# Attention keys stored window by window, gate loads and bias set-up at other times, and the gate multiplied into half of the output weights

## The chip, the cores and the metric

The kernel runs on one core of one Trainium2 chip. The metric is device time in microseconds (us) of one execution, as the median of several runs. A profile is one further execution, recorded by the hardware profiler; it is read through views (groups of instructions by line, waits, timelines, sums over windows, the chain that ended last). The five engines are TensorE (PE; its weight loads are listed as PEld), VectorE (DVE), ScalarE (ACT), GpSimd (POOL) and SyncE (SP), whose queue issues most DMAs.

## What is computed

One layer of a backbone with three kinds of heads, for 1024 latent tokens (a grid of 16 rows x 64 columns), 256 context tokens and width 1024:

```
mod   = silu(c) @ w_ada + b_ada;  shift, scale, gate = split(mod, 3)
h     = rmsnorm(x, norm_g) * (1 + scale) + shift          # the same for ctx, with c_ctx
z     = h @ w_in                                          # 3840 columns, cut into 11 parts
ya    = z_b * conv3(z_c * z_h) * silu(z_g)                # 256 columns
yb    = attention(q, k, v, k_ctx, v_ctx, rpb) * silu(z_g) # 8 heads of 64
yc    = silu(layernorm(conv31(z_p * sigmoid(z_q)))) * silu(z_g)
out   = rmsnorm(x + gate * (concat(ya, yb, yc) @ w_out), final_g)
```

In the attention each latent query sees a clamped window of 8 rows x 16 columns of the grid, with a learned bias by head, row and column distance (rpb), and all 256 context keys, in one softmax with scale 1/8.

## The kernel before

**Arithmetic.** Every float32 operand of a large product is split into a high part, rounded to the fp32r type, and the rest (`split`, L129 and L130: the high part on ACT, the subtraction on POOL or DVE). A product is then three matmuls: high x high, high x low, low x high.

**Order of the work.** The program is Python that unrolls into one instruction list. PE's order is the order of the program text. In the first stage DVE, ACT, POOL and SP also follow the text; after it a scheduler orders these four, by the order of the text and its own estimate of when operands are ready. Each engine then executes its list strictly in order, waiting at the first instruction whose operands are missing.

- *Start (0 to 66 us).* The string `SEQ` is the written order: each word is a letter for a function in `start` with its arguments. `L` loads a part of w_ada, `X` a token tile, `W` half of a weight block of w_in, `w` splits it (`split_w`, ACT then POOL), `q`, `r`, `x` make the RMS norm, `B` multiplies by w_ada (L220), `R` copies that row out of PSUM (ACT, L225), `C` turns it into columns and makes scale and shift (PE transposes L232, DVE L234 to L240), `a`, `b`, `c` are PE transposes of normed tokens (L279), `f`, `g`, `h` apply scale and shift (ACT, L294), `u`, `v`, `o` split the result (DVE, L300 and L301), `m`, `n` are the query and key products of head pair 0 (L1009 to L1012), `Q` stores them, and `D` issues matmuls on zeros that keep PE going.
- *Values and set-up (66 to 163 us).* `build` runs the first conformer projection, the context keys of pair 0 and the value projection (`v_proj`, L412 to L414, ten tiles of 24 matmuls) on PE. Beside them run coroutines. `spawn(gen, delay)` adds one; `run` issues PE work and advances a planned clock `now` by an estimate for each product; `poll` lets those coroutines issue a step whose time has come. `v_weights` splits the value weights. `ada_gates` loads 16 pieces of the gate columns of w_ada (L809), sums them on DVE (L812, L814), splits the sum and stores it to DRAM (`gd`, L822). `bias_first` makes the bias tables of the first head: DMAs through DRAM (L445) into seven arrays `u`, then 21 loads into the tables `bt` (L502). `conv_part(31, 1.6)` issues the first 31 of 62 taps of the 31-wide convolution on DVE (L685). `drain()` issues all that is left before attention starts. The pool `t2` has four buffers: the loads and split halves of `ada_gates` and the value tiles that leave PSUM (ACT L423, DVE L424, stored by L425) take them in turn. PSUM holds three projection results (`ps_z`).
- *Attention (163 to 486 us).* For each of four head pairs: queries and keys are projected, then 16 blocks (2 heads x 8 blocks of 16 rows x 8 columns of queries) run with other projections in between. `sink_k` writes the keys times -1/8 into `kt[:, h]`, the high part in 64 partitions and the rest in the other 64 (ACT L371, DVE L372), token after token. `scores` multiplies a block of 128 queries by 2 or 3 column groups of keys (`kwin`, L589) and by the context keys (L590), twice each (queries high and low). The 256 or 384 window keys are read as 16 rows x 8 columns for each group: runs of 8 numbers, 64 apart.
- *Output (486 to 616 us).* `load_wout` loads a half of w_out (512 columns) in four pieces of 128x1024 through two buffers `fraw` and splits them (ACT, POOL; L130, tile `wol`). Half 0 is loaded first, then the y tiles, then half 1, all ahead of the output matmuls. `out_mm` makes 24 matmuls for a tile of 128 tokens (L867 to L869); the first four tiles of half 0 run on six of eight channel blocks first, then `gate_rows` broadcasts the gate row to all partitions (PE L836, DVE L838), then the rest. `out_part` multiplies a result by the gate (DVE L883), adds x (L884) and makes the sum of squares (ACT L890; DVE L886 for the last 256 columns); `out_gain` multiplies by final_g on POOL (L894); `out_mean` and `out_scale` make 1/rms on POOL (L900, L902, L909, L910) and scale and store the tile (L913 to L921).

Of the kernel before, what the change touches and what calls it, by code (L numbers as in the profile page):

```python
# [16 lines left out]
P = 128  # L17
D = 1024
# [33 lines left out]
X0 X1 X2 X3 L00 K L01 W00 W10 L10 L11 X4 X5 X6 X7 W01 W11 L20 L21 L30 L31 X8 X9  # L52
q00 q11 r02 q20 x0 x1 q31 r22 x2 x3 D29 B00 D02 B01 a0 R0 a1 w00 w10 C0 a22 D07
f0 f1 a3 u0 u1 m0 B10
# [7 lines left out]
def f32(ap):  # L62
    return ap.bitcast(F32)


class Builder:
# [236 lines left out]

    def load_w(self, src):
        return [w for g in range(2) for w in self.split_w(self.load_wraw(src, g))]

# [5 lines left out]

    def split_w(self, wr):
        hk = KT // 2
        wh = self.wp.tile([P, hk, P], F32R, name="wh", tag="wh")
        wl = self.wp.tile([P, hk, P], F32R, name="wl", tag="wl")
        self.split(wh, wl, wr, self.nc.gpsimd)
        return [(wh[:, i], wl[:, i]) for i in range(hk)]
# [17 lines left out]
    def proj_lat(self, c0, sink, ctx=False, w=None):  # L336
        if w is None:
            w = self.load_w(self.a["w_in"][:, c0:c0 + P])
            for half in range(2):
                yield from self.proj(w, half * HALF, HALF, lambda ps: sink(half, ps))  # L340
        if ctx:
            yield from self.proj(w, T, TC, lambda ps: sink(2, ps))
        yield 0
# [18 lines left out]

    def sink_k(self, half, ps, heads=(0, 1)):
        nc = self.nc
        t0, n = half * HALF, ps.shape[1]
        s = -QSCALE
        for h in heads:
            own = slice(64 * h, 64 * h + 64)
            oth = slice(64 - 64 * h, 128 - 64 * h)
            kk = self.kt[:, h, t0:t0 + n]  # L370
            nc.scalar.activation(out=kk[own], in_=ps[own], func=AF.Copy, scale=s)  # L371
            nc.vector.scalar_tensor_tensor(out=kk[oth], in0=ps[own], scalar=s, in1=f32(kk[own]),  # L372
                                           op0=ALU.mult, op1=ALU.subtract)

# [201 lines left out]
    def scores(self, kt, h, b, qv):  # L576
# [272 lines left out]

    def load_wout(self, half, pool):  # L850
        wh = pool.tile([P, KT, HALF], F32R, name=f"woh{half}")
        wl = pool.tile([P, KT, HALF], F32R, name=f"wol{half}")
        for q in range(4):
            raw = self.fr.tile([P, 2, HALF], F32, name="fraw")
            src = self.a["w_out"][q * 256:(q + 1) * 256, half * HALF:(half + 1) * HALF]
            self.nc.sync.dma_start(out=raw, in_=src.rearrange("(k p) n -> p k n", p=P))
            self.split(wh[:, 2 * q:2 * q + 2], wl[:, 2 * q:2 * q + 2], raw, self.nc.gpsimd)
        return wh, wl
# [18 lines left out]
    def out_part(self, tt, cs, j, ps, lp, eng):  # L877
# [4 lines left out]
        g = lp.tile([P, HALF], F32, name="fg", bufs=2)[:, 0:n]  # L882
        nc.vector.tensor_tensor(out=g, in0=ps[:, 0:n], in1=self.gate[:, cs], op=ALU.mult)  # L883
        nc.vector.tensor_tensor(out=xt[:, cs], in0=g, in1=xt[:, cs], op=ALU.add)  # L884
        if eng is nc.vector:
            nc.vector.tensor_tensor_reduce(g, xt[:, cs], xt[:, cs], op0=ALU.mult, op1=ALU.add, scale=1.0, scalar=0.0,  # L886
                                           accum_out=ss[:, j:j + 1])
        else:
# [16 lines left out]
    def out_scale(self, tt, j, parts):  # L905
        nc = self.nc
        xt, ss = self.xres[tt]
        r, s = ss[:, 3:4], ss[:, j - 1:j]
        nc.gpsimd.tensor_scalar(out=r, in0=ss[:, j:j + 1], scalar1=1.0 / D, scalar2=s, op0=ALU.mult, op1=ALU.add)  # L909
        nc.gpsimd.tensor_tensor(out=r, in0=r, in1=self.mhalf[:, 0:1], op=ALU.pow)  # L910
# [13 lines left out]
    def start(self, zb, attn_pool):  # L924
# [22 lines left out]

        def w(i, g):
            ws[i][4 * g:4 * g + 4] = self.split_w(wr.pop((i, g)))

# [80 lines left out]
    def build(self):  # L1031
# [53 lines left out]
        self.spawn(self.v_weights(stv.enter_context(self.pool("vw", 1, side="right"))), 2.0)  # L1085
        self.spawn(self.ada_gates(), 5.0)
        self.spawn(self.bias_first(), 10.0)
        first = self.cf_in(0)
        self.run(itertools.islice(first, KT), self.proj_pair(0, self.ws[1]), first)
        self.conv = self.cf_conv()  # L1090
        self.spawn(self.conv_part(31, 1.6))
        self.run(self.v_proj())
        self.drain()
        stv.close()
# [20 lines left out]
        with ExitStack() as st:  # L1115
# [76 lines left out]
```

## Time and profile before

| | |
|---|---|
| median of 3 runs | 619.52 us (618.75 to 619.55) |
| profiled execution, its own time | 617.89 us |
| span of its instructions | 616.1 us |
| instructions in the profile | 8935, of them 3101 matmuls |
| bytes read from and written to HBM | 55.93 MB and 14.29 MB |
| mean granted TensorE clock | 0.995 of full speed |

The profile's page gives, for each engine, the time in which it had an instruction under way, its share of the span and the count. The end of a matmul is modelled, and matmuls overlap, so the time from one start to the next says more than the duration. A row of a timeline reads: start, duration, engine, line, operation, out<-in, shape, count; in square brackets stands how long the engine sat idle before it and what it waited for. A row of a windows view gives each engine's busy time and count in a stretch, then the granted clock (PEclk), the busy share of the DMA engines and GB/s. A row of groups gives busy time, the mean in ns of one, and the idle time before them with the releaser.

### The profile page before, as it was taken

The page shows a single profiled execution, that of the slowest core. Times are in us where ns is not written, and L with a number is a line of the kernel's source. Part 1 is how long each engine was busy: PE and PEld are TensorE (multiplying, and loading weights), DVE is VectorE, ACT ScalarE, POOL GpSimd, SP SyncE. Part 2 cuts the span into 40 slices and gives each one's busy share as a digit, 9 for nine tenths or more (in the row PEclk, how much of TensorE's full clock was granted, in tenths as well). Part 3 has the DMA queues.
Part 4 walks back from the last instruction along what each step waited for, and adds up shares of the span by engine and source line. Part 5 has one row for each costly group of instructions (what it writes and reads, how often), then busy time and mean ns, then how long its engine had stood idle before and what let it go on. Part 6 is the DMA issues. An engine that isn't in the chain of part 4 may idle for free.

```text
span 616.1 us, 8935 instructions
## 1 busy us (share of the span) xinstructions
PE 593.8 (96%) x3101; PEld 497.0 (81%) x3101; DVE 401.1 (65%) x682; ACT 244.0 (40%) x468; POOL 178.4 (29%) x199
## 2 busy tenths in 40 slices
PE   7799999899999999999999999999999999999995
PEld 5467887688888888888888888888788888888884
DVE  4466977798356589577797666836879456352433
ACT  2455812111255542455523554424645434331222
POOL 1231112300233221424322433313434270265112
PEclk9999999899999999999999999999999999999998
DMA  8991658965623117331146242172311455770122
GB/s 286 357 326 41 222 151 175 158 173 160 164 49 93 37 55 202 75 86 49 28 136 141 48 113 55 36 222 52 82 28 35 133 151 160 273 272 1 70 102 103
DMA packets 97171, 78.64 MB, mean 128 GB/s; under 512 B 26508, under 2 KB 80870, under 8 KB 96998
## 3 DMA queue, kind: packets, MB, share of 16 engines
q1 hardware_dynamic: 95397, 71.51, 41.6%
q10 hardware_dynamic: 1728, 6.55, 3.0%
q8 instruction: 25, 0.41, 0.3%
q14 instruction: 21, 0.16, 0.1%
HBM read 55.93 MB, written 14.29 MB: 114 GB/s over the span
## 4 chain that ended last, share of the span: by engine, by line
PE 82%; DVE 6%; DMA 4%; ACT 2%; issue 2%; SPq 1%; POOL 1%; DVEq 0%; POOLq 0%; ACTq 0%
PE ps_z L324 13%; PE ps_z L326 13%; PE ps_z L325 13%; PE po L620 5%; PE ps_t L608 5%; PE ps_f L868 5%; PE ps_f L869 5%; PE ps_f L867 5%; PE ps_s L589 4%; DMA t<-in_w_ada 2%; PE ps_s L590 2%; PE ps_z L412 2%; PE ps_z L414 2%; PE ps_z L413 2%; DMA wa<-in_w_ada 2%
## 5 line engine op out<-in xcount | busy, mean ns | idle before, releaser
L324 PE MATMUL ps_z<-h,wh 128*128 128x512 f32 x384 | 151.1, 394 | 0.0
L326 PE MATMUL ps_z<-h,wl 128*128 128x512 f32 x384 | 150.2, 391 | 0.0
L325 PE MATMUL ps_z<-h,wh 128*128 128x512 f32 x384 | 149.7, 390 | 0.0
L130 POOL TENSOR_TENSOR wl<-wr,wh 128x512 fp32r<-128x512 f32 x52 | 71.8, 1384 | 146.8 <-ACT wh L129 118.0
L599 POOL TENSOR_SCALAR pr<-pr,sm 128x640 f32<-128x640 f32 (+1 forms) x64 | 52.9, 827 | 138.0 <-DVE sm L598 117.2
L326 PEld LDWEIGHTS ps_z<-h,wl 128*128 128x128 f32 x384 | 72.1, 188 | 16.1
L685 DVE SCALAR_TENSOR_TENSOR acc<-t,half_w,acc 128x1024 f32<-128x1024 f32 x60 | 83.0, 1384 | 1.0
L325 PEld LDWEIGHTS ps_z<-h,wh 128*128 128x128 f32 x384 | 72.2, 188 | 12.4
L324 PEld LDWEIGHTS ps_z<-h,wh 128*128 128x128 f32 x384 | 72.2, 188 | 12.1
L612 ACT ACTIVATE pw<-ps_t 128x640 fp32r<-128x640 f32 (+1 forms) x64 | 43.5, 680 | 90.7 <-PE ps_t L608 90.6
L594 DVE CUSTOM_DVE_ANT_0 ps_s<-ps_s,bt 128x640 f32<-128x640 f32 (+1 forms) x64 | 51.0, 796 | 33.7 <-PE ps_s L590 31.0
L613 DVE TENSOR_TENSOR pw<-ps_t,pw 128x640 fp32r<-128x640 f32 (+1 forms) x64 | 50.4, 788 | 17.3 <-ACT pw L612 16.9
L597 ACT ACTIVATE pr<-ps_s,mn 128x640 f32<-128x640 f32 (+1 forms) x64 | 49.0, 766 | 20.2 <-DVE mn L594 19.2
L620 PE MATMUL po<-pw,vt 128*128 128x256 f32 x304 | 51.3, 297 | 2.0 <-DVE yb L571 1.0
L868 PE MATMUL ps_f<-wol,y 128*128 128x512 f32 (+1 forms) x136 | 51.6, 379 | 0.0
L869 PE MATMUL ps_f<-woh,y 128*128 128x512 f32 (+1 forms) x136 | 51.5, 379 | 0.0
L867 PE MATMUL ps_f<-woh,y 128*128 128x512 f32 (+1 forms) x136 | 51.5, 379 | 0.0
L129 ACT ACTIVATE wh<-wr 128x512 fp32r<-128x512 f32 x52 | 32.5, 629 | 34.9 <-PE ps_z L325 20.9
L608 PE MATMUL ps_t<-ident,pr 128*128 128x128 f32 x304 | 43.6, 272 | 0.0
L620 PEld LDWEIGHTS po<-pw,vt 128*128 128x128 f32 x304 | 40.4, 189 | 3.8 <-issue 3.4
L589 PE MATMUL ps_s<-kt,qd 128*128 128x384 f32 (+1 forms) x128 | 42.2, 351 | 0.5 <-ACT pr L597 0.4
L608 PEld LDWEIGHTS ps_t<-ident,pr 128*128 128x128 f32 x304 | 36.0, 142 | 1.8 <-issue 0.9
(171 smaller groups left out, 911.4 us busy)
## 6 DMA issues: line engine op xcount, KB each, us to landing
wr<-in_w_in SPq DMA_DIRECT2D x52, 256.0 KB
wa<-in_w_ada SPq DMA_DIRECT2D x16, 512.0 KB
qd<-qn SPq DMA_DIRECT2D x32, 256.0 KB
vd<-t SPq DMA_DIRECT2D x20, 256.0 KB
x_in<-in_x SPq DMA_DIRECT2D x8, 512.0 KB
t<-in_w_ada SPq DMA_DIRECT2D x16, 256.0 KB
vt<-vd SPq DMA_DIRECT2D x32, 128.0 KB
fraw<-in_w_out SPq DMA_DIRECT2D x8, 512.0 KB
```

What stands on the lines that cost most here:

```text
L130: i2 = (eng or nc.vector).tensor_tensor(out=lo, in0=src, in1=f32(hi), op=ALU.subtract)
L324: nc.tensor.matmul(ps, lhsT=wh, rhs=hh, start=(k == 0), stop=False)
L325: nc.tensor.matmul(ps, lhsT=wh, rhs=hl, start=False, stop=False)
L326: self.last = nc.tensor.matmul(ps, lhsT=wl, rhs=hh, start=False, stop=(k == KT - 1))
L589: nc.tensor.matmul(win, lhsT=q[:, b % 4], rhs=kwin, start=(i == 0), stop=(i == 1))
L599: nc.gpsimd.tensor_scalar(out=pr, in0=pr, scalar1=sm, scalar2=0.5, op0=ALU.mult, op1=ALU.mult)
L608: nc.tensor.transpose(out=pt[:, c * P:(c + 1) * P], in_=pr[:, c * P:(c + 1) * P], identity=self.ident)
L620: self.nc.tensor.matmul(po, lhsT=vt[:, vi, h], rhs=pw[:, c], start=(c == 0), stop=(c == n - 1))
L685: self.after_pe(nc.vector.scalar_tensor_tensor(out=acc, in0=u[:, t:t + T], scalar=self.half_w[:, 2 * t + ct:2 * t + ct + 1], in1=acc, op0= ...
L867: nc.tensor.matmul(ps, lhsT=yh, rhs=wh[:, ch], start=(first and i == 0), stop=False)
L868: nc.tensor.matmul(ps, lhsT=yh, rhs=wl[:, ch], start=False, stop=False)
L869: nc.tensor.matmul(ps, lhsT=yl, rhs=wh[:, ch], start=False, stop=(last and i == len(chs) - 1))
```

## The change

1. **Keys.** `kt[:, h, 0:1024]` is stored group by group: eight groups of 128 keys, each 16 rows x 8 columns, so that `kwin` is one contiguous run. `sink_k` writes with that permutation. The factor -1/8 moves into the key weights: `split_w` applies it (ACT on the high part, then DVE in place of POOL for the rest); for pair 0 a further ACT instruction in `w` scales the raw weights.
2. **Start.** The first splits of the query and key weights (`w00 w10` in `SEQ`) become `w001`, placed ahead of `R0`, and `w101`, placed after `a1`; the last digit 1 sends their subtraction to DVE instead of POOL. `w01` and `w11` stay on POOL.
3. **Set-up.** `ada_gates` starts at 1.0 instead of 5.0 on the planned clock, `bias_first` at 22 instead of 10, the gap between convolution taps is 2.2 instead of 1.6, and the `drain()` after the value projection is gone.
4. **Output.** Half 1 of w_out is loaded after `gate_rows`, and each piece is multiplied in place by the gate on POOL before it is split. `out_part` of that half omits the multiplication on DVE. For the last 256 columns the sum of squares takes the earlier sum as its start value and 1/1024 as its scale, so that one POOL instruction of `out_scale` goes.

```diff
-q00 ... D29 B00 D02 B01 a0 R0 a1 w00 w10 C0 a22 D07
+q00 ... D29 B00 D02 B01 a0 w001 R0 a1 w101 C0 a22 D07
...
+    def split_w(self, wr, scale=None, eng=None):
         wh = self.wp.tile([P, hk, P], F32R, name="wh", tag="wh")
         wl = self.wp.tile([P, hk, P], F32R, name="wl", tag="wl")
-        self.split(wh, wl, wr, self.nc.gpsimd)
+        if scale is None:
+            self.split(wh, wl, wr, eng or self.nc.gpsimd)
+        else:
+            self.nc.scalar.activation(out=wh, in_=wr, func=AF.Copy, scale=scale)
+            self.nc.vector.scalar_tensor_tensor(out=wl, in0=wr, scalar=scale, in1=f32(wh), op0=ALU.mult, op1=ALU.subtract)
...
     def sink_k(self, half, ps, heads=(0, 1)):
-            kk = self.kt[:, h, t0:t0 + n]
-            nc.scalar.activation(out=kk[own], in_=ps[own], func=AF.Copy, scale=s)
-            nc.vector.scalar_tensor_tensor(out=kk[oth], in0=ps[own], scalar=s, in1=f32(kk[own]),
-                                           op0=ALU.mult, op1=ALU.subtract)
+            if half < 2:
+                kk = self.kt[:, h, 0:T].rearrange("p (g r c) -> p r g c", g=NB, c=BW)[:, 8 * half:8 * half + 8]
+                src = ps.rearrange("p (r g c) -> p r g c", g=NB, c=BW)
+            else:
+                kk, src = self.kt[:, h, T:], ps
+            nc.scalar.activation(out=kk[own], in_=src[own], func=AF.Copy)
+            nc.vector.tensor_tensor(out=kk[oth], in0=src[own], in1=f32(kk[own]), op=ALU.subtract)
...
-        kwin = kt[:, h, 0:T].rearrange("p (r g c) -> p g r c", g=NB, c=BW)[:, g0:g0 + ng]
+        kwin = kt[:, h, g0 * GK:(g0 + ng) * GK]
...
     def load_wout(self, half, pool, gate=None):
...
             self.nc.sync.dma_start(out=raw, in_=src.rearrange("(k p) n -> p k n", p=P))
+            if gate is not None:
+                self.nc.gpsimd.tensor_tensor(out=raw, in0=raw, in1=gate.unsqueeze(1).to_broadcast([P, 2, HALF]),
+                                             op=ALU.mult)
...
-        nc.vector.tensor_tensor(out=g, in0=ps[:, 0:n], in1=self.gate[:, cs], op=ALU.mult)
-        nc.vector.tensor_tensor(out=xt[:, cs], in0=g, in1=xt[:, cs], op=ALU.add)
+        if j == 0:
+            nc.vector.tensor_tensor(out=g, in0=ps[:, 0:n], in1=self.gate[:, cs], op=ALU.mult)
+            nc.vector.tensor_tensor(out=xt[:, cs], in0=g, in1=xt[:, cs], op=ALU.add)
+        else:
+            nc.vector.tensor_tensor(out=xt[:, cs], in0=ps[:, 0:n], in1=xt[:, cs], op=ALU.add)
...
+            nc.vector.tensor_tensor_reduce(g, xt[:, cs], xt[:, cs], op0=ALU.mult, op1=ALU.add, scale=1.0 / D,
+                                           scalar=ss[:, j - 1:j], accum_out=ss[:, j:j + 1])
...
+        def w(i, g, e=0):
+            t = wr.pop((i, g))
+            if i:
+                S.activation(out=t, in_=t, func=AF.Copy, scale=-QSCALE)
+            ws[i][4 * g:4 * g + 4] = self.split_w(t, eng=(G, V)[e])
...
-        self.spawn(self.ada_gates(), 5.0)
-        self.spawn(self.bias_first(), 10.0)
+        self.spawn(self.ada_gates(), 1.0)
+        self.spawn(self.bias_first(), 22.0)
...
-        self.spawn(self.conv_part(31, 1.6))
+        self.spawn(self.conv_part(31, 2.2))
         self.run(self.v_proj())
-        self.drain()
...
-            w1 = self.load_wout(1, lp)
...
                         self.gate_rows(ps_g)
+                        w1 = self.load_wout(1, lp, self.gate[:, HALF:])
```

More of the change, by code (lines that the diff above doesn't have):

```diff
@@ L52 @@
 X0 X1 X2 X3 L00 K L01 W00 W10 L10 L11 X4 X5 X6 X7 W01 W11 L20 L21 L30 L31 X8 X9
-q00 q11 r02 q20 x0 x1 q31 r22 x2 x3 D29 B00 D02 B01 a0 R0 a1 w00 w10 C0 a22 D07
+q00 q11 r02 q20 x0 x1 q31 r22 x2 x3 D29 B00 D02 B01 a0 w001 R0 a1 w101 C0 a22 D07
 f0 f1 a3 u0 u1 m0 B10
@@ L301, in h_split, with load_w @@
         nc.vector.tensor_tensor(out=lo, in0=raw, in1=f32(hi), op=ALU.subtract)
-    def load_w(self, src):
-        return [w for g in range(2) for w in self.split_w(self.load_wraw(src, g))]
+    def load_w(self, src, scale=None):
+        return [w for g in range(2) for w in self.split_w(self.load_wraw(src, g), scale)]
     def load_wraw(self, src, g):
@@ L311, in load_wraw @@
         return wr
-    def split_w(self, wr):
+    def split_w(self, wr, scale=None, eng=None):
         hk = KT // 2
@@ L337, in proj_lat @@
         if w is None:
-            w = self.load_w(self.a["w_in"][:, c0:c0 + P])
+            w = self.load_w(self.a["w_in"][:, c0:c0 + P], -QSCALE if ctx else None)
             for half in range(2):
@@ L364, in sink_k @@
         nc = self.nc
-        t0, n = half * HALF, ps.shape[1]
-        s = -QSCALE
         for h in heads:
@@ L848, in load_y, with load_wout @@
         self.split(*self.y[ch], raw)
-    def load_wout(self, half, pool):
+    def load_wout(self, half, pool, gate=None):
         wh = pool.tile([P, KT, HALF], F32R, name=f"woh{half}")
@@ L882, in out_part @@
         g = lp.tile([P, HALF], F32, name="fg", bufs=2)[:, 0:n]
-        nc.vector.tensor_tensor(out=g, in0=ps[:, 0:n], in1=self.gate[:, cs], op=ALU.mult)
-        nc.vector.tensor_tensor(out=xt[:, cs], in0=g, in1=xt[:, cs], op=ALU.add)
+        if j == 0:
[3 more added lines that the diff above has]
+            nc.vector.tensor_tensor(out=xt[:, cs], in0=ps[:, 0:n], in1=xt[:, cs], op=ALU.add)
         if eng is nc.vector:
-            nc.vector.tensor_tensor_reduce(g, xt[:, cs], xt[:, cs], op0=ALU.mult, op1=ALU.add, scale=1.0, scalar=0.0,
-                                           accum_out=ss[:, j:j + 1])
+            nc.vector.tensor_tensor_reduce(g, xt[:, cs], xt[:, cs], op0=ALU.mult, op1=ALU.add, scale=1.0 / D,
+                                           scalar=ss[:, j - 1:j], accum_out=ss[:, j:j + 1])
         else:
@@ L908, in out_scale @@
         r, s = ss[:, 3:4], ss[:, j - 1:j]
-        nc.gpsimd.tensor_scalar(out=r, in0=ss[:, j:j + 1], scalar1=1.0 / D, scalar2=s, op0=ALU.mult, op1=ALU.add)
+        if j == 1:
+            nc.gpsimd.tensor_scalar(out=r, in0=ss[:, j:j + 1], scalar1=1.0 / D, scalar2=s, op0=ALU.mult, op1=ALU.add)
+        else:
+            r = ss[:, j:j + 1]
         nc.gpsimd.tensor_tensor(out=r, in0=r, in1=self.mhalf[:, 0:1], op=ALU.pow)
@@ L946, in W @@
             wr[i, g] = self.load_wraw(a["w_in"][:, 1024 + 512 * i:1152 + 512 * i], g)
-        def w(i, g):
-            ws[i][4 * g:4 * g + 4] = self.split_w(wr.pop((i, g)))
+        def w(i, g, e=0):
[3 more added lines that the diff above has]
+            ws[i][4 * g:4 * g + 4] = self.split_w(t, eng=(G, V)[e])
         def q(i, e):
@@ L1132, in build @@
             ps_g = e(self.pool("ps_g", 2, PSUM, side="right"))
-            w1 = self.load_wout(1, lp)
             self.xres = []
             sync, act, half0 = nc.sync.dma_start, nc.scalar.dma_start, slice(0, HALF)
-            for half, w in ((0, w0), (1, w1)):
+            w = w0
+            for half in range(2):
+                if half:
+                    w = w1
                 for t0 in (0, 4):
```

## The prediction, made before the change was run

> **What bounds the kernel now.** I read the page first, then sums over stretches of the span, then PE's waits.
>
> ```profile
> span 616.1 us, 8935 instructions
> PE 593.8 (96%) x3101; PEld 497.0 (81%) x3101; DVE 401.1 (65%) x682; ACT 244.0 (40%) x468; POOL 178.4 (29%) x199
> 526.00:616.00 90.00, 83.11 (x385) 68.65 (x383) 34.03 (x49) 21.98 (x45) 30.20 (x38) 0.98 0.38 138
> ```
>
> PE is the bound: it is idle for 616.1 - 593.8 = 22.3 us in all. So there are only two ways to gain: take away PE's idle time, or make its own instructions shorter. In the third row (stretch, length, then busy time of PE, PEld, DVE, ACT, POOL) 6.9 us of the idle time lie in the output; the other engines work there after the last matmul. PE's waits name two more that this change can reach:
>
> ```profile
> PE ps_z L412 <- DVE t L424: 3.1, 1, 3.1
> PE ps_h L279 <- ACT h_raw L294: 1.2, 1, 1.2
> ```
>
> **Set-up: the 3.1 us wait.** The timeline of PE around it, and the sum of that stretch:
>
> ```profile
> 106.15 0.40 PE L414 MATMUL ps_z<-wv,h 128*128 128x512 f32 x1
> 109.66 0.47 PE L412 MATMUL ps_z<-wv,h 128*128 128x512 f32 x1 [3.11 <-DVE t L424]
> ...
> 110.89 0.51 PE L414 MATMUL ps_z<-wv,h 128*128 128x512 f32 x1
> ...
> 114.54 0.40 PE L414 MATMUL ps_z<-wv,h 128*128 128x512 f32 x1
> 114.77 0.40 PE L412 MATMUL ps_z<-wv,h 128*128 128x512 f32 x1
> 106.00:115.00 9.00, 5.89 (x19) 4.37 (x18) 8.96 (x11) 2.17 (x5) 2.10 (x1) 0.81 0.96 188
> ```
>
> At full clock a 512-wide matmul starts 0.23 us after the one before (the last pair). From 106.15 to 109.66 is 3.51 us: 3.28 lost. From 110.89 to 114.54 are nine starts in 3.65 us instead of 2.07: 1.58 more lost, since the granted clock falls after the stall (mean 0.81 in this stretch). The wait costs 4.86 us, not 3.1.
>
> Its cause, followed back: a value tile could not leave PSUM, since the gate's chain held its `t2` buffer.
>
> ```profile
> 95.21 3.26 SPq L809 DMA_DIRECT2D t<-in_w_ada  x1
> 101.16 0.75 DVE L814 SCALAR_TENSOR_TENSOR acc<-t,stat,acc 128x512 f32<-128x512 f32 x1 [2.46 <-DMA t<-in_w_ada]
> 106.07 0.39 ACT L423 ACTIVATE t<-ps_z 128x256 fp32r<-128x256 f32 x1 [1.75 <-DMA gd<-t]
> L814 DVE SCALAR_TENSOR_TENSOR acc<-t,stat,acc 128x512 f32<-128x512 f32 x14 | 11.2, 815 | 7.6 <-DMA t<-in_w_ada 7.5
> ```
>
> A value tile is 24 x 0.23 = 5.5 us of PE and the third ends at 106.4, so the first was ready at 95.4; it moves at 106.07, after the gate's store. The last gate load is issued at 95.21 and the last sum starts at 101.16. The 14 sums lose 7.5 us to loads that share SP's queue with the bias DMAs. The change starts the gate four planned microseconds earlier (4.2 us of real time: the text plans 0.65 for three matmuls that take 0.69), moves the bias DMAs 12.7 us back, out of the loads' way, and thins the taps on DVE. So the chain moves by 4.2 to 4.2 + 7.5 = 11.7 us, and the buffers come free at 94.4 to 101.9 instead of 106.07. PE needs its fourth `ps_z` at 106.4, and a value half leaves PSUM by steps of 0.4 us on ACT and DVE: it fits at both ends, with 2 us to spare at the worse one. I take all of it, -4.9; if some stall stays and only the after-effect goes, it is -1.6. The gate's sums now stand ahead of the splits of the value weights on DVE, which is in order: a split can wait behind a gate load as L814 did, 2.46 us. The splits are for tiles that PE reaches at 90 at the earliest, so the price is 0 as long as the loads keep the pace.
>
> The bias DMAs are moved past the value stores, on SP.
>
> ```profile
> 156.31 1.35 SPq L359 DMA_DIRECT2D qd<-qn  x2
> ```
>
> The first queries were issued at 156.31 at 0.68 us each; attention will want them 4.9 us earlier. From 106 to 151 the text issues on SP 18 value stores, 7 loads into `u`, 21 into the tables, 9 of values and some 6 others: 61 x 0.68 = 41 us of 45. That just fits, so I cost it at nothing; without that cover PE waits for the queries (rival 2). POOL's fills for the tables move with them, ahead of nothing that PE needs. Some seven taps move beside the gate projection and the first attention blocks, on a DVE that is busy 65% of the span: nothing.
>
> **Start: -0.6 us.**
>
> ```profile
> 17.74 1.14 ACT L129 ACTIVATE wh<-wr 128x512 fp32r<-128x512 f32 x2
> 18.44 2.53 POOL L130 TENSOR_TENSOR wl<-wr,wh 128x512 fp32r<-128x512 f32 x2 [5.47 <-ACT wh L129]
> 18.98 0.76 DVE L238 TENSOR_TENSOR scl<-ada_t,modc 128x4 f32<-128x4 f32 x1
> 19.77 1.22 DVE L240 TENSOR_TENSOR scl<-scl,modc 128x4 f32<-128x4 f32 x1
> 21.09 1.45 ACT L294 ACTIVATE h_raw<-ps_h,shift,scl 128x512 f32<-128x512 f32 x2 [2.21 <-DVE scl L240]
> 23.42 0.69 DVE L301 TENSOR_TENSOR h<-h_raw,h 128x512 fp32r<-128x512 f32 x1
> 28.45 0.16 DVE L240 TENSOR_TENSOR scl<-scl,modc 128x4 f32<-128x4 f32 x1
> ```
>
> L238 and L240 handle four numbers a partition and took 0.76 and 1.22 us while POOL ran its two subtractions; at 28 us, with POOL idle, L240 took 0.16. With the subtractions on DVE the two lose 1.66 us. Against it: ACT gets a third step (1.14 / 2 = 0.57), one cast now ahead of `R0`, and DVE gets a subtraction (0.69, as L301) ahead of the reduction. The second weight half had landed by 18.3, when its cast ran. If it lands by 17.9, scaling and cast end at 19.0, the subtraction at 19.7, the reduction and its three small steps at 20.4, instead of 20.99: -0.6. If it lands only at 18.3 and the cast ahead delays `R0` by its 0.57: +0.3. If ACT waits for nothing: -0.9. PE waited 1.2 us for this step, and its list of waits has no load of the later start stage, so the shift carries through. `w11` gains the same 0.57 us on ACT later, with no PE wait near: 0.
>
> **Keys.** Groups by shape:
>
> ```profile
> L324 PE MATMUL ps_z<-h,wh 128*128 128x512 f32 x384 | 151.1, 394 | 0.0
> L590 PE MATMUL ps_s<-kt,qd 128*128 128x256 f32 x128 | 36.3, 288 | 0.0
> L589 PE MATMUL ps_s<-kt,qd 128*128 128x384 f32 x96 | 33.6, 371 | 0.5 <-ACT pr L597 0.4
> L324 PE MATMUL ps_z<-hc,wh 128*128 128x256 f32 x32 | 9.0, 280 | 0.0
> L589 PE MATMUL ps_s<-kt,qd 128*128 128x256 f32 x32 | 8.6, 292 | 0.0
> ```
>
> A contiguous 384-wide matmul should lie between 280 and 394 ns: 337, or 345 with the 8 ns that L590, already contiguous, has over 280. L589 takes 371: 26 ns x 96 = 2.5 us, 2.0 without the waits in its row. But its 256-wide form, also in runs of eight, has only 4 ns over L590; scaled to three groups 6 ns x 96 = 0.6 us. I take the middle, -1.3; bounds 0 and -3.3 (34 ns x 96). [...]
>
> The permuted write of the keys costs nothing: queries are written in such a pattern already.
>
> ```profile
> L372 DVE SCALAR_TENSOR_TENSOR kt<-ps_z,kt 64x512 fp32r<-64x512 f32 x14 | 9.6, 689 | 10.2 <-ACT kt L371 9.8
> L353 DVE TENSOR_TENSOR qn<-ps_z,qn 128x512 fp32r<-128x512 f32 x8 | 5.5, 690 | 1.4 <-ACT qn L352 1.3
> ```
>
> Six subtractions for key weights move from POOL to DVE, into projections where PE waits for neither: 0 (bounds -0.3 and +0.3, half of one such step).
>
> **Output.** After the last matmul:
>
> ```profile
> 609.15 0.42 DVE L883 TENSOR_TENSOR fg<-ps_f,gate 128x256 f32<-128x256 f32 x1 [0.80 <-PE ps_f L869]
> 609.61 0.43 DVE L884 TENSOR_TENSOR xres<-fg,xres 128x256 f32<-128x256 f32 x1
> 609.74 0.43 POOL L902 TENSOR_SCALAR fss<-fss 128x1 f32<-128x1 f32 x1
> 610.67 0.27 POOL L909 TENSOR_SCALAR fss<-fss 128x1 f32<-128x1 f32 x1 [0.51 <-DVE fss L886]
> 611.02 0.55 POOL L910 TENSOR_TENSOR fss<-fss,mhalf 128x1 f32<-128x1 f32 x1
> ```
>
> L883 goes (0.46 to the next start) and L909 goes (0.35): -0.8. The added wait: L886 now needs L902, which ends at 610.17. But the chain to L902 loses an L883 in tile 6 and one in tile 7 and ends near 609.1, before L886 starts at 609.6. Behind L886 on DVE only the last scalings are queued. Without that shift the gain would be 0.1, the upper bound.
>
> Half 1 gets four multiplications on POOL and starts after the gate.
>
> ```profile
> 536.63 1.29 DVE L838 TENSOR_TENSOR gate<-ps_g,gate 128x512 f32<-128x512 f32 x2 [8.51 <-PE ps_g L836]
> L130 POOL TENSOR_TENSOR wol<-fraw,woh 128x1024 fp32r<-128x1024 f32 x8 | 19.2, 2416 | 38.0 <-ACT woh L129 38.0
> L894 POOL TENSOR_TENSOR xres<-xres,fgam 128x512 f32<-128x512 f32 x8 | 10.3, 1292 | 0.6
> 570.01 0.69 DVE L883 TENSOR_TENSOR fg<-ps_f,gate 128x512 f32<-128x512 f32 x1 [4.17 <-PE ps_f L869]
> ```
>
> From 537.9, 8 x 2.42 = 19.3 us of POOL, and some 2 us for a load between the two pairs of pieces: ready at 559. The first tile of half 1 ends at 570.0, so with 24 x 0.23 us it starts at 564.5. That is 5.5 us of cover: cost 0.
>
> **Sum.** -4.9 - 0.6 - 1.3 - 0.8 = -7.6 us against the profiled execution's 617.89: 610.3. That one ran 1.6 us under the median of 619.52, so the median becomes 611.9. All bounds at once give -10.2 to -1.1, 609.3 to 618.4; the upper ends are of unrelated terms and will hardly meet.
>
> **Rivals.**
> 1. Keys gain nothing, the rest as forecast: -6.3, 613.2. For it: the 256-wide row. Against: the 371 ns.
> 2. A new wait at the start of attention, for queries behind the bias DMAs on SP: about as long as the old one, so about 4.9 us with the clock's after-effect: -2.7, 616.8. For it: 41 of 45 us. Against: the late tables of the last block can wait longer than the queries.
> 3. Slower: the weights of half 1 come too late. It decides if POOL's list holds the eight L894 ahead of the last split (8 x 1.29 = 10.3 us) and the loads wait as much again as assumed (4 us in place of 2, with two to three more for the small steps between): ready at about 574, 9.5 us after PE's need, and 1.6 us of lower clock: 11.1 - 7.6 = +3.5, 623.0. From an extra delay of 11.5 us on it is slower. Against: the loads stand ahead of the L894 in the text.
> 4. The wait at 106 us stays, as another user of the four buffers holds them: -2.7, 616.8. Against: the row of L423 names the gate's store.
>
> **Chances.** Forecast 0.52, rival 1 0.20, rival 2 0.14, rival 4 0.06, rival 3 0.08. A measurement of this kernel can tell about 0.2%, 1.2 us, from no change. Rivals 2 and 4 may meet poor ends of the other terms, which gives 0.05 within 0.2%. So faster 0.87, same 0.05, slower 0.08. The range takes in rivals 2 and 4: 609.2 to 617.0.
>
> **What would show it.** Right: no PE wait at L412, the granted clock at full from 66 to 163 us, the last L814 before 98; L240 at 0.16 us near 20; the 384-wide L589 at 345 ns; 0.8 us less from the last matmul's start to the end. Wrong: PE waits at L589 near 158 for a query load, at L867 near 560 for `wol`, or L589 still at 371.

## The result, and the profile after

The changed kernel took 611.42 us, the median of 4 executions from 610.97 to 612.36; the kernel before, timed beside it, took 619.13. The ratio is 0.9878, with a 95% interval of 0.9861 to 0.9895. In a later series the same two kernels gave 611.52 and 617.90, ratio 0.9893 [0.9876, 0.9910]. The prediction was 611.9. The profiled execution took 610.97 us with a span of 609.2. Most line numbers are some lines higher than before: PE's L412, L589, L590, L620 and L869 are now L419, L596, L597, L627 and L879.

Busy time by engine, from the page (instructions behind the x), and PE's waits (from what, on what, us in total, times, longest):

```profile
PE 589.7 (97%) x3101; PEld 493.8 (81%) x3101; DVE 400.7 (66%) x681; ACT 245.9 (40%) x470; POOL 182.1 (30%) x194
```

```profile
PE po L627 <- DVE yb L578: 3.1, 4, 1.0
...
PE po L627 <- ACT pw L619: 0.8, 1, 0.8
```

The wait on `t` at L419 is gone, `h_raw` halved, and a wait on `yb` has grown: 3.1 us in four places, where the same view of before had 1.0 us in two (at L620, on L571). Of the four only the one at 304.56, of 1.03 us, is new. Two others stood under `yb` before as well, and the one at 440.36 (0.86 us) was there with 0.81 us, put down to `pw`. The 0.8 us put down to `pw` now is the other new wait, at 174.81. PE is busy 4.1 us less, and idle 2.8 us less. Busy time alone would mislead here: of the 4.1 us only a part is shorter matmuls, as the slow clock behind the old stall counted as busy (there, at 111.20, a 512-wide matmul took 0.63 us, against 0.40 at 114.54).

Both kernels issue the same 3101 matmuls in the same order, so the n-th start of one can be set against the n-th of the other. The difference of the two, read at the ends of the stages, is a ledger of where time went (in the changed kernel's time the set-up ends at 156 us, just ahead of the first query-key matmul):

| stretch, in the changed kernel's time | predicted | measured |
|---|---|---|
| start, to 28 us | -0.6 | -0.86 |
| set-up, 28 to 156 us | -4.9 | -5.44 |
| attention, 156 to 486 us | -1.3 | +0.11 |
| 486 us to the last matmul | 0 | 0.00 |
| last matmul to the end | -0.8 | -0.73 |
| sum | -7.6 | -6.92 |

The two profiled executions stood 1.2 and 0.5 us under their medians, so the medians differ by 7.7 and the spans by 6.9. The total was close; attention, where the keys were to gain, gave nothing.

**Set-up.** The stretch of the old stall, and three steps of the gate and the queries in order of time:

```profile
106.00:115.00 9.00, 9.00 (x41) 7.40 (x40) 7.36 (x9) 1.32 (x4) 0.00 (x0) 1.00 1.04 113
```

```profile
94.23 0.74 DVE L821 SCALAR_TENSOR_TENSOR acc<-t,stat,acc 128x512 f32<-128x512 f32 x1
...
97.38 0.38 ACT L430 ACTIVATE t<-ps_z 128x256 fp32r<-128x256 f32 x1 [1.74 <-DMA gd<-t]
...
149.10 1.33 SPq L364 DMA_DIRECT2D qd<-qn  x2
```

PE is busy for all 9 us, with 41 matmuls where it had 19, at a granted clock of 1.00 instead of 0.81. The last gate sum moved from 101.16 to 94.23, and the first value tile leaves PSUM at 97.38 instead of 106.07. The queries go out at 149.10, 7.7 us before the first query-key matmul at 156.8.

**Start.** DVE's small steps, and the PE step that waits for them:

```profile
19.79 0.17 DVE L238 TENSOR_TENSOR scl<-ada_t,modc 128x4 f32<-128x4 f32 x1
...
19.98 0.16 DVE L240 TENSOR_TENSOR scl<-scl,modc 128x4 f32<-128x4 f32 x1
...
21.07 0.66 PE L279 MATMUL ps_h<-ident,x_in 128*128 128x128 f32 x4 [0.56 <-ACT h_raw L294]
```

L238 and L240 took 0.17 and 0.16 us instead of 0.76 and 1.22.

**Keys.** Query-key matmuls by shape (count, then busy us and mean ns):

```profile
L597 PE MATMUL ps_s<-kt,qd 128*128 128x256 f32 x128 | 35.2, 281 | 0.0
L596 PE MATMUL ps_s<-kt,qd 128*128 128x384 f32 x96 | 31.3, 348 | 0.5 <-ACT pr L604 0.4
...
L596 PE MATMUL ps_s<-kt,qd 128*128 128x256 f32 x32 | 8.3, 280 | 0.0
```

All three are shorter, from 288, 371 and 292 ns; the 384-wide one came out 3 ns from the 345 that the prediction took. L597 reads the context keys, which were contiguous before: it gained all the same, and experiment 1 shows that it is the window's layout that makes the difference.

**What gave the keys' gain back.** The ledger has two large steps in attention, +1.03 at the matmul at 174.81 and +1.27 at 304.56. The timeline there, after and then before:

```profile
171.90 1.27 DVE L692 SCALAR_TENSOR_TENSOR acc<-t,half_w,acc 128x1024 f32<-128x1024 f32 x1
...
174.25 0.41 DVE L578 TENSOR_TENSOR yb<-po,yb 64x256 f32<-64x256 f32 x1
...
174.81 0.83 PE L627 MATMUL po<-pw,vt 128*128 128x256 f32 x5 [0.80 <-ACT pw L619]
...
300.76 0.68 DVE L322 SCALAR_TENSOR_TENSOR wl<-wr,wh 128x512 fp32r<-128x512 f32 x1
...
302.67 1.29 DVE L692 SCALAR_TENSOR_TENSOR acc<-t,half_w,acc 128x1024 f32<-128x1024 f32 x1
303.99 0.43 DVE L578 TENSOR_TENSOR yb<-po,yb 64x256 f32<-64x256 f32 x1
...
304.56 0.83 PE L627 MATMUL po<-pw,vt 128*128 128x256 f32 x5 [1.03 <-DVE yb L578]
```

```profile
179.18 0.42 DVE L571 TENSOR_TENSOR yb<-po,yb 64x256 f32<-64x256 f32 x1
...
180.32 0.84 PE L620 MATMUL po<-pw,vt 128*128 128x256 f32 x5
...
308.82 0.43 DVE L571 TENSOR_TENSOR yb<-po,yb 64x256 f32<-64x256 f32 x1
...
309.74 0.84 PE L620 MATMUL po<-pw,vt 128*128 128x256 f32 x5
```

`po` is freed by DVE's addition into `yb`. Before, it was done 0.7 and 0.5 us ahead of the matmul; now the matmul starts 0.15 us after its end. At 174 the thinner convolution taps have left a tap in attention (L692) on DVE; at 303 a key weight's subtraction (L322) that POOL did before pushes the next tap ahead of the addition. The first wait is put down to ACT's `pw` in the row, but the matmul also starts 0.15 us after L578's end, as at 304, and the run with denser taps below settles it.

**Output.** The last matmul and what follows:

```profile
602.64 0.28 PE L879 MATMUL ps_f<-woh,y 128*128 128x256 f32 x1
...
603.53 0.48 DVE L901 CUSTOM_DVE_ANT_0 fg<-xres,fss 128x256 f32<-128x256 f32 x1
...
604.11 0.55 POOL L928 TENSOR_TENSOR fss<-fss,mhalf 128x1 f32<-128x1 f32 x1 [1.47 <-DVE fss L901]
```

From the last matmul's start to the end of the span are 6.54 us, where they were 7.27. POOL, with half 1's weights:

```profile
531.96 5.23 POOL L865 TENSOR_TENSOR fraw<-fraw,gate 128x1024 f32<-128x1024 f32 x2 [31.27 <-DMA xres<-in_x]
...
555.07 1.29 POOL L909 TENSOR_TENSOR xres<-xres,fgam 128x512 f32<-128x512 f32 x1
556.33 2.42 POOL L130 TENSOR_TENSOR wol<-fraw,woh 128x1024 fp32r<-128x1024 f32 x1
```

The last piece is ready at 558.75; half 1 starts at 558.04 and first reads that piece at 561.07, in its fourteenth matmul. PE waits for nothing.

### The profile page after: what moved, and what is told of

The parts are those of the page before. It is cut to its first block, busy times and chain, and to the rows that moved or that the text cites. A ratio compares the mean times of both kernels' runs of the same rounds, so it can differ in the third digit from the quotient of the medians.

```text
span 609.2 us, 8937 instructions
## 1 busy us (share of the span) xinstructions
PE 589.7 (97%) x3101; PEld 493.8 (81%) x3101; DVE 400.7 (66%) x681; ACT 245.9 (40%) x470; POOL 182.1 (30%) x194
## 4 chain that ended last, share of the span: by engine, by line
PE 84%; DVE 5%; ACT 3%; issue 2%; DMA 2%; POOL 2%; SPq 1%; POOLq 0%; DVEq 0%; ACTq 0%
PE ps_z L329 14%; PE ps_z L331 14%; PE ps_z L330 14%; PE po L627 5%; PE ps_f L878 5%; PE ps_f L879 5%; PE ps_f L877 5%; PE ps_t L615 4%; PE ps_z L419 3%; PE ps_z L421 3%; PE ps_s L596 3%; PE ps_z L420 3%; PE ps_s L597 2%; DMA wr<-in_w_in 2%; PE ps_h L279 1%
## 5 line engine op out<-in xcount | busy, mean ns | idle before, releaser
L130 POOL TENSOR_TENSOR wl<-wr,wh 128x512 fp32r<-128x512 f32 x44 | 60.8, 1384 | 167.3 <-ACT wh L129 160.3
L606 POOL TENSOR_SCALAR pr<-pr,sm 128x640 f32<-128x640 f32 (+1 forms) x64 | 56.6, 884 | 138.2 <-DVE sm L605 118.1
L692 DVE SCALAR_TENSOR_TENSOR acc<-t,half_w,acc 128x1024 f32<-128x1024 f32 x60 | 81.1, 1351 | 1.2
L620 DVE TENSOR_TENSOR pw<-ps_t,pw 128x640 fp32r<-128x640 f32 (+1 forms) x64 | 50.4, 788 | 16.0 <-ACT pw L619 15.8
L627 PE MATMUL po<-pw,vt 128*128 128x256 f32 x304 | 51.3, 297 | 4.1 <-DVE yb L578 3.1
L879 PE MATMUL ps_f<-woh,y 128*128 128x512 f32 (+1 forms) x136 | 51.5, 379 | 0.0
L129 ACT ACTIVATE wh<-wr 128x512 fp32r<-128x512 f32 x46 | 29.0, 630 | 42.3 <-PE ps_z L330 21.0
L627 PEld LDWEIGHTS po<-pw,vt 128*128 128x128 f32 x304 | 40.5, 189 | 6.4 <-issue 4.7
L596 PE MATMUL ps_s<-kt,qd 128*128 128x384 f32 (+1 forms) x128 | 39.6, 331 | 0.5 <-ACT pr L604 0.4
```

Of the source, the lines that this page charges most:

```text
L130: i2 = (eng or nc.vector).tensor_tensor(out=lo, in0=src, in1=f32(hi), op=ALU.subtract)
L596: nc.tensor.matmul(win, lhsT=q[:, b % 4], rhs=kwin, start=(i == 0), stop=(i == 1))
L606: nc.gpsimd.tensor_scalar(out=pr, in0=pr, scalar1=sm, scalar2=0.5, op0=ALU.mult, op1=ALU.mult)
L627: self.nc.tensor.matmul(po, lhsT=vt[:, vi, h], rhs=pw[:, c], start=(c == 0), stop=(c == n - 1))
L692: self.after_pe(nc.vector.scalar_tensor_tensor(out=acc, in0=u[:, t:t + T], scalar=self.half_w[:, 2 * t + ct:2 * t + ct + 1], in1=acc, op0= ...
L879: nc.tensor.matmul(ps, lhsT=yl, rhs=wh[:, ch], start=False, stop=(last and i == len(chs) - 1))
```

## The experiments

Every run is the changed kernel with the edit shown. "Net" is the ledger against the changed kernel between the two times given, so it leaves out where the first load happens to land (0 to 1.4 us between executions, all before 16 us). In each series the kernel before was timed too: its medians were 618.62 (key layout, drain, key weights on POOL with ACT, runs of 32 to 1), 617.90 (denser taps, the best version, bias alone) and 618.92 (one execution, beside the last four).

The changed kernel itself went once more beside the second of these, for comparison:

> The changed kernel as it is, timed on the same chip as the next three, so that they can be set against it: 0.988 of the time before.

It took 611.52 us (610.79 to 612.09) with a span of 609.3, and the ledger stays within some 0.2 us of the first profile from 16 us on.

**1. The old key layout.**

```
-            if half < 2:
-                kk = self.kt[:, h, 0:T].rearrange("p (g r c) -> p r g c", g=NB, c=BW)[:, 8 * half:8 * half + 8]
+            kk, src = self.kt[:, h, half * HALF:half * HALF + ps.shape[1]], ps
...
-        kwin = kt[:, h, g0 * GK:(g0 + ng) * GK]
+        kwin = kt[:, h, 0:T].rearrange("p (r g c) -> p g r c", g=NB, c=BW)[:, g0:g0 + ng]
```

> The changed kernel with the keys stored token after token again, so that the window is read in runs of 8 as before; all else as changed. Theory (each new run costs TensorE about 0.5 ns, whatever the line): the 384-wide window matmul goes from 178 ns to the next start back to 194, the context matmul behind it from 117 to 125, in all 2.7 us more: 614.1 us. [...]

614.21 us (5 runs), ratio 0.9930 [0.9918, 0.9942]; net +2.1 us from 115 to 486, in small steps through all four attention pairs. Its groups:

```profile
L593 PE MATMUL ps_s<-kt,qd 128*128 128x256 f32 x128 | 36.3, 288 | 0.0
L592 PE MATMUL ps_s<-kt,qd 128*128 128x384 f32 x96 | 33.6, 370 | 0.5 <-ACT pr L600 0.4
L592 PE MATMUL ps_s<-kt,qd 128*128 128x256 f32 x32 | 8.6, 292 | 0.0
```

The old means are back, on all three shapes. The layout is worth 2.1 us, and rival 1 (no gain) is out. With 2.1 gained and 1.03 + 1.27 lost, the ledger's +0.1 comes out to within 0.1; the largest of the small steps that are left is -0.27 at L734.

**2. The taps as dense as before, and the drain ahead of attention.**

```
-        self.spawn(self.conv_part(31, 2.2))
+        self.spawn(self.conv_part(31, 1.6))
         self.run(self.v_proj())
+        self.drain()
```

> The changed kernel with the gap between taps at 1.6 again and the issue of all that is left ahead of attention; gate and bias keep their new times. Theory (the first new wait in attention, 1.0 us at 174 us, is VectorE held by a tap): it goes, and the time falls by 1.0 us to 610.4. Rival (the wait comes from TensorE being early, or moves on): the wait stays, the time stays at 611.4 or, if the bias loads issued at once hold up the queries, rises by 1 to 3 us.

617.71 us (12 runs), ratio 0.9985 [0.9974, 0.9997]: nearly the whole gain was gone, net +7.0 by 163 us and -1.04 at the matmul at 174. The queue and PE at the start of attention, and the stretch after it:

```profile
156.56 3.50 SPq L364 DMA_DIRECT2D qd<-qn  x4
...
161.23 0.55 PE L596 MATMUL ps_s<-kt,qd 128*128 128x256 f32 x1 [4.24 <-DMA qd<-qn]
```

```profile
161.00:168.00 7.00, 6.77 (x22) 5.76 (x23) 1.73 (x5) 0.78 (x2) 0.69 (x1) 0.58 0.65 150
```

The queries went out at 156.56, not 149.10, behind the table loads that the drain had issued first; PE waited 4.24 us and then ran at a clock of 0.58. That is rival 2. Two edits differ here, the drain and the taps; experiment 3 has the taps alone.

**3. The denser taps without the drain.** Only the first of those two lines.

> The changed kernel with the gap between taps at 1.6 again, and still without the issue of all that is left ahead of attention. The run with both put back lost 4.2 us to a query load and, in its trace, no longer had the wait at 174 us. Theory (the tap gap alone makes that wait, the early issue alone made the query late): no query wait, no wait at 174 us, 1.0 us faster than the changed kernel (0.986 of before). Rival (taps that stand closer crowd the value stage and bring back part of the old wait): a wait at L419 near 107 us, same or slower than the changed kernel.

611.00 us, ratio 0.9881 [0.9867, 0.9896], against 611.52 for the changed kernel in that series. The same place as at 174 above, some 1.3 us later by the start:

```profile
173.96 0.42 DVE L578 TENSOR_TENSOR yb<-po,yb 64x256 f32<-64x256 f32 x1
...
175.06 0.84 PE L627 MATMUL po<-pw,vt 128*128 128x256 f32 x5
...
175.40 0.71 ACT L619 ACTIVATE pw<-ps_t 128x640 fp32r<-128x640 f32 x1 [0.78 <-PE ps_t L615]
```

No tap stands ahead of L578, and PE waits for nothing: net -1.07 from 163 to 243 us. PE starts here before the `pw` step that the changed kernel's row named, so that step was not its releaser. By the medians alone the gain is within what can be told; the place is plain in the trace. No wait for queries came, so in experiment 2 the drain was needed for it; the drain behind the thin taps was not run.

**4. The key weights' subtraction back on POOL, ACT scaling first.**

```
-            self.nc.scalar.activation(out=wh, in_=wr, func=AF.Copy, scale=scale)
-            self.nc.vector.scalar_tensor_tensor(out=wl, in0=wr, scalar=scale, in1=f32(wh), op0=ALU.mult, op1=ALU.subtract)
+            self.nc.scalar.activation(out=wr, in_=wr, func=AF.Copy, scale=scale)
...
+        self.split(wh, wl, wr, eng or self.nc.gpsimd)
```

> The changed kernel with the subtraction for the key weights of pairs 1 to 3 on GpSimd again (ScalarE scales the raw weights in place first); the key layout stays. Theory (the second new wait in attention, 1.2 us at 303 us, is VectorE held by that subtraction): it goes, the time falls by 1.1 us to 610.3. Rival (a tap holds VectorE there and the subtraction only happens to stand beside it): the wait stays at about 1.2 us and the time at 611.4.

612.49 us (5 runs), ratio 0.9905 [0.9892, 0.9917]. The wait at 303 went (-1.27), but with ACT's added step three others grew at query-key matmuls: +0.45 at 196, +0.56 at 281 and +0.72 at 367 us. PE's wait there for ACT's `pr` rose from 0.4 us to 2.0. The cause of the wait at 303 is confirmed, and the repair only moved it.

**5. Denser taps, and the key weights scaled and subtracted on POOL.**

```
-            self.nc.scalar.activation(out=wh, in_=wr, func=AF.Copy, scale=scale)
-            self.nc.vector.scalar_tensor_tensor(out=wl, in0=wr, scalar=scale, in1=f32(wh), op0=ALU.mult, op1=ALU.subtract)
+            self.nc.gpsimd.tensor_scalar(out=wr, in0=wr, scalar1=scale, scalar2=None, op0=ALU.mult)
...
+        self.split(wh, wl, wr, eng or self.nc.gpsimd)
...
-        self.spawn(self.conv_part(31, 2.2))
+        self.spawn(self.conv_part(31, 1.6))
```

> As the run before, and the key weights of pairs 1 to 3 scaled and subtracted on GpSimd (one more GpSimd instruction each; ScalarE only rounds). Theory: both new attention waits go and ScalarE gets no new work, so 2.1 us faster than the changed kernel (0.984 of before). Rival (GpSimd, with two instructions for each key weight half, delays the probabilities of the attention behind them): the wait at 303 us is replaced by one for GpSimd or ScalarE, and it is no faster than the run before.

609.62 us (609.44 to 609.77), ratio 0.9860 [0.9845, 0.9875]: the fastest of all, 1.9 us under the changed kernel beside it. Net -2.6 from 163 to 486 us. The place at 303:

```profile
302.36 0.43 DVE L576 TENSOR_TENSOR yb<-po,yb 64x256 f32<-64x256 f32 x1
...
303.22 0.84 PE L625 MATMUL po<-pw,vt 128*128 128x256 f32 x5
```

The addition is again ahead of the matmul, by 0.4 us. Both losses in attention came from work that the change put on DVE there: the first is gone when the taps are issued earlier, the second when POOL, busy 30% of the changed kernel's span, takes the subtraction.

**6. What took the 106 us stall away: only the bias set-up back at 10, only the gate's start back at 5, both back.**

```
-        self.spawn(self.bias_first(), 22.0)
+        self.spawn(self.bias_first(), 10.0)
```

```
-        self.spawn(self.ada_gates(), 1.0)
+        self.spawn(self.ada_gates(), 5.0)
```

> The changed kernel with only the bias set-up at its old time (10 planned us in place of 22); the gate stays early, the taps apart. Theory (the gate's loads were late since they shared the queue with the bias DMAs): a wait at L419 near 107 us of 1 to 3 us comes back, 1 to 4.5 us longer. Rival (the gate's own early start is what counts): no such wait, 0 to 0.5 us.

> The changed kernel with the gate's loads spawned at 5.0 again; the bias set-up stays at 22. In the run with only the bias put back to 10 the wait at L419 stayed away, so the question is whether the gate's early start is needed at all. Theory A, the early start alone does it: without it the gate's chain ends about 4.2 us later than in the changed kernel and as late as before, so a PE wait on DVE t at L419 of 2 to 3.3 us comes back near 106 us, with slow clock behind it: 3.5 to 5.5 us against the changed kernel by 120 us. Theory B, either of the two alone does it: with no bias load among them the gate's loads are issued faster, the last L821 starts near 98.4, the buffer is free at about 101.6 and PE wants it at 105.5: no wait, within 0.3 us of the changed kernel at 120 us, net of the start.

> The changed kernel with both put back: gate loads at 5.0 and bias set-up at 10. The thinner taps (2.2) and the missing drain stay. If gate and bias together made the stall (theory A or B): the wait on DVE t is back near 106 us, about 3 us long, and the program loses 4.5 to 5.5 us by 120 us. If the taps on DVE were what held the gate's sums back (rival): no wait or one of under 1 us, under 1.5 us lost.

One execution each: 611.98, 611.57 and 612.74 us. Net from 66 to 115 us: +0.3, 0.0 and +1.7. The gate's sums in the three, one fence for each (count, shortest, median and longest ns, first and last start):

```profile
L821 DVE SCALAR_TENSOR_TENSOR acc<-t,stat,acc x14: 730/747/1767, 77.5 to 96.3; 128x512 f32<-128x512 f32 x14
```

```profile
L821 DVE SCALAR_TENSOR_TENSOR acc<-t,stat,acc x14: 734/743/1718, 77.8 to 96.2; 128x512 f32<-128x512 f32 x14
```

```profile
L821 DVE SCALAR_TENSOR_TENSOR acc<-t,stat,acc x14: 731/751/1718, 77.5 to 100.1; 128x512 f32<-128x512 f32 x14
```

Either of the two alone ends the sums near 96 and no wait comes; only with both back do they end at 100.1 and PE waits. That wait, and the clock of its stretch, in the third:

```profile
107.28 0.47 PE L419 MATMUL ps_z<-wv,h 128*128 128x512 f32 x1 [1.49 <-DVE t L431]
```

```profile
105.00:115.00 10.00, 8.51 (x38) 6.70 (x37) 6.38 (x8) 2.34 (x6) 1.19 (x2) 1.00 0.98 159
```

It is half as long as the old one, and the clock did not fall. So putting back both brings back 1.7 of the 5.4 us. The rest hangs on what still differs from the kernel before: the taps' density, the drain and the earlier start among others. The rows point to the taps: before, a tap at 104.74 stood ahead of the gate's second split and of the first value sum, and here both run earlier. What shortens the stall when the times are the old ones was not tried by a run of its own, and stays open.

For the new times experiment 2 is the other side of the test. It has gate and bias at their new times but the taps and the drain as before, and its net is 0.0 from 28 to 156 us, with no wait at L419 and the clock at full until attention:

```profile
66.00:158.00 92.00, 90.99 (x411) 75.10 (x409) 73.43 (x91) 23.77 (x46) 15.91 (x20) 1.00 0.73 180
```

So the new times of gate and bias are enough for the whole gain of the set-up, without the thin taps.

**7. The old start and the old output, in one kernel, as they lie 580 us apart.**

```
-... B01 a0 w001 R0 a1 w101 C0 a22 D07
+... B01 a0 R0 a1 w00 w10 C0 a22 D07
...
+            w1 = self.load_wout(1, lp)
...
-                        w1 = self.load_wout(1, lp, self.gate[:, HALF:])
...
-        if j == 0:
+        if True:
             nc.vector.tensor_tensor(out=g, in0=ps[:, 0:n], in1=self.gate[:, cs], op=ALU.mult)
...
-        if j == 1:
+        if True:
             nc.gpsimd.tensor_scalar(out=r,
```

> The changed kernel with two parts put back that lie far from each other: the start's weight splits in the old order, on POOL, and the output as before (gate multiplied in for both halves by DVE, half 1's weights loaded before the gate, the mean square finished by POOL). The set-up, the keys and the taps stay. Theory, each part is worth what the comparison of before and after gives: 0.4 to 0.6 us lost between 16 and 28 us, with L240 (the same line here as before or a few lines further) at about 1.2 us beside POOL's subtractions, and from the last matmul's start to the end 7.2 to 7.3 us in place of 6.54. Rival: POOL's subtractions do not slow the small DVE steps, they were slow for another reason: no loss at the start. Rival for the output: the four multiplications on POOL cost PE something at 558 us: then this run gains there, by up to 0.5 us.

613.07 us, one execution. The steps at both places:

```profile
18.72 2.54 POOL L130 TENSOR_TENSOR wl<-wr,wh 128x512 fp32r<-128x512 f32 x2 [5.52 <-ACT wh L129]
19.26 0.76 DVE L238 TENSOR_TENSOR scl<-ada_t,modc 128x4 f32<-128x4 f32 x1
...
20.06 1.22 DVE L240 TENSOR_TENSOR scl<-scl,modc 128x4 f32<-128x4 f32 x1
...
22.20 0.66 PE L279 MATMUL ps_h<-ident,x_in 128*128 128x128 f32 x4 [1.20 <-ACT h_raw L294]
...
605.81 0.27 POOL L924 TENSOR_SCALAR fss<-fss 128x1 f32<-128x1 f32 x1 [0.79 <-DVE fss L900]
```

L238 and L240 are back at 0.76 and 1.22 us, to the hundredth, PE loses 0.64 at L279, and the ledger 0.58 from 16 to 28 us. POOL's two subtractions run beside them again, and L240 ends at 21.28, 0.02 us after the second one; the order of ACT's steps went back too, and was not tried apart. From the last matmul's start to the end it takes 7.58 us, 1.03 more than the changed kernel; 0.28 of that is that POOL starts L924 0.79 us after it fell idle where the kernel before showed 0.51, so the output's part is worth some 0.7 to 1.0. Half 1's weights, loaded early again, gain nothing at 558 us.

**8. What the read pattern costs.** Windows read in other orders, by pair of heads:

```
+        run = (32, 4, 2, 1)[self.pair]
+        kwin = kt[:, h, g0 * GK:(g0 + ng) * GK].rearrange("p (x y c) -> p y x c", y=64 // run, c=run)
```

```
+        run, y = ((8, 8), (8, 2), (16, 4), (2, 2))[self.pair]
+        kwin = kt[:, h, g0 * GK:(g0 + ng) * GK].rearrange("p (x y c) -> p y x c", y=y, c=run)
```

> The changed kernel with the window keys read in another order, in which the length of a contiguous run differs by head pair: 32, 4, 2 and 1 numbers for pairs 0 to 3, runs 64 numbers apart. The attention then mixes up the keys of a window, so the output is not the reference's; all shapes and counts are kept. By start times of the 384-wide window matmul and the context matmul behind it, 295 ns together with one run and 319 with runs of 8. Theory (0.5 ns for each run): 301, 343, 391 and 487 ns. [...]

> Attention mixes keys here: the windows read as many numbers as before, in other places, so the output is not the reference's. Pairs 0 to 3 read runs of 8 numbers 64 apart (as the kernel before), 8 numbers 16 apart, 16 numbers 64 apart, and 2 numbers 4 apart. So far the sum of a 384-wide window and a context matmul, start to start, was 296 ns contiguous and for runs of 32, 321 for 8 at 64, 330 for 4, 522 for 2, 362 for 1, all of these 64 apart. Theory jump: a run's start costs when the next run is far away, so 8 at 16 apart comes to 296 to 305, and 2 at 4 apart to under 400. Theory count: only the number of runs counts, so 8 at 16 apart gives 321 and 2 at 4 apart 522 again. Runs of 16 should lie between 296 and 321 by both, near 308 if the cost goes with the number of runs.

Median from the start of a 384-wide window matmul past its context matmul to the next start:

| run of numbers, apart | ns |
|---|---|
| contiguous (changed kernel) | 296 |
| 8, 64 apart, through all 1024 (old layout) | 321 |
| 8, 64 apart, through 384 | 299 |
| 8, 16 apart | 292 |
| 16, 64 apart | 300 |
| 32, 64 apart | 296 |
| 4, 64 apart | 330 |
| 2, 64 apart | 522 |
| 2, 4 apart | 468 |
| 1, 64 apart | 362 |

Three starts of the changed kernel, and three of the first of these runs with numbers by twos:

```profile
172.72 0.33 PE L596 MATMUL ps_s<-kt,qd 128*128 128x384 f32 x1
172.89 0.28 PE L597 MATMUL ps_s<-kt,qd 128*128 128x256 f32 x1
173.01 0.34 PE L596 MATMUL ps_s<-kt,qd 128*128 128x384 f32 x1
```

```profile
340.57 0.56 PE L598 MATMUL ps_s<-kt,qd 128*128 128x384 f32 x1
340.94 0.31 PE L599 MATMUL ps_s<-kt,qd 128*128 128x256 f32 x1
341.10 0.56 PE L598 MATMUL ps_s<-kt,qd 128*128 128x384 f32 x1
```

No theory held. A price for each run makes single numbers the worst, and they were cheaper than twos (362 against 522 ns); nearer runs made eights free (292 ns at 16 apart) and twos hardly cheaper (468 at 4 apart); and the same eights, 64 apart, cost 25 ns in the old layout and 3 when they go through 384 numbers only. That the old layout costs 25 ns here is shown, by what rule is open.

## Why the prediction came out, point by point

**Set-up, -4.9 against -5.4: right in size, and the cause holds, but its parts do not add up.** The chain moved to 97.38, inside the bounds given, and the slow clock went with the stall as said: the two were worth 5.0 in the ledger, and a short pause of before, at 122.72, most of the rest. But the prediction counted the gate's start and the bias DMAs as adding up; experiment 6 shows that each alone is enough with the thin taps and no drain, and experiment 2 that both together are enough without these. With both put back and the taps thin, only 1.7 us of the 5.4 is lost again, and what saves the rest there is not shown.

**Queries behind the bias loads, 0 against 0.** The queue fitted. Rival 2 was a real one: with the taps at 1.6, one line, the drain, separates the two outcomes by some 6 us in the medians (617.71 and 611.00, from two series).

**Start, -0.6 against -0.57 from 16 to 28 us.** The other 0.29 of the ledger came before 16 us, where executions differ by chance, by 0 to 1.4 us.

**Keys, -1.3 against -2.1: right in kind, too small.** The term was mis-sized: it took the context matmuls as the fixed measure, and they gained as well. From start to start, experiment 1 against the changed kernel, the 96 window matmuls of 384 went from 194 to 178 ns (1.5 us), the context matmuls gave 1.0 us and the 256-wide windows 0.3. Of these 2.7 us 2.1 reached the ledger; the rest came back as waits. That the 384-wide rows alone had given an estimate of 2.0 is in part luck. The lower bound, 0, which is rival 1, does not hold for this read: 321 against 296 ns. For the same runs through 384 numbers, 299 ns, it nearly does.

**Taps and key subtractions, 0 against +2.3: wrong.** The steps that failed are "on a DVE that is busy 65% of the span: nothing" and "Six subtractions ... into projections where PE waits for neither: 0". The busy share is an average; where one DVE step frees `po` with 0.5 us to spare, a tap of 1.3 us ahead of it is a wait. The subtraction wasn't waited for itself: it moved a tap, and the tap moved the addition. Experiment 3 shows the first, 4 the second, and 5 both together. No rival had this mechanism.

**Output, -0.8 against -0.73.** As worked out, and L901 did not wait for L917.

**Half 1's weights, 0 against 0, but the cover was wrong.** In the changed kernel's own time the prediction had them ready near 553 (559 less the 6.2 that came before); it was 558.75, since three of the eight `fgam` multiplications did stand ahead on POOL and each gate multiplication took 2.6 us. The last piece came 0.7 us after half 1's start, by which the prediction had reckoned its 5.5 us of cover; what saved it is that this piece is first read 3.0 us into the tile, so the cover was 2.3 us. Rival 3 came that close.

That the total came so near is luck in part: the keys' and set-up's extra 1.3 us, with a start 0.3 better, paid for most of the 2.3 that was missed.

## What to carry to other kernels

When work moves to an in-order engine, look not at its busy share but at the steps on it that free a buffer for the bound engine, and at how much each has to spare; here a step of 0.7 us that nobody waited for pushed another one past that point. Where two edits both take pressure off one stall, undo them one at a time and then together: here, with the taps thinned, either was enough. A row's named releaser need not be the one that counted (at 174.81 it was `pw`, and in experiment 3 the same matmul started 0.34 us ahead of that step): set the matmul's start against the ends of all that it needs.

## What the runs showed of the hardware

Beside POOL's 128x512 subtractions, small DVE steps (4 numbers in each partition) took 0.76 and 1.22 us instead of 0.16, in both kernels that have them there; where DVE makes the subtractions itself, the same steps take 0.17 and 0.16. It was no fixed price for each step. Later in the kernel before, at 52.95, L238 ran beside such a subtraction and took 0.20 us:

```profile
51.86 1.28 POOL L130 TENSOR_TENSOR wl<-wr,wh 128x512 fp32r<-128x512 f32 x1 [11.25 <-ACT wh L129]
...
52.95 0.20 DVE L238 TENSOR_TENSOR scl<-ada_t,modc 128x4 f32<-128x4 f32 x1
```

In all these rows the step ends 0.01 to 0.02 us after a subtraction on POOL does: at 53.15 and 53.14 here; near 20 us in the kernel before L240 at 20.99 and the second subtraction at 20.97, and L238 at 19.74 and the first, if it took the 1.28 us of this one, at 19.72. So in these rows a step took as long as the subtraction still had to run when it started: 0.74, 1.20 and 0.19 us were left, and the steps took 0.76, 1.22 and 0.20.

The granted clock fell after PE waits of 3.11 and 4.24 us (kernel before, 0.81 from 106 to 115 us; experiment 2, 0.58 from 161 to 168) and stayed at 1.00 after one of 1.49 (experiment 6, both put back, 105 to 115).

Reading the window keys in runs of two numbers, 64 apart, cost more than single numbers (522 against 362 ns), which none of the theories here foretold.
